# Attention and delta outputs split into two parts where they are made, in a one-core decoder layer on Trainium2

## The chip, the cores and the metric

One core of one Trainium2 chip runs the whole kernel. The time is device microseconds (us) of one execution of the program; the figure of a kernel is the median of several runs. Engines in the rows: PE is TensorE, PEld its weight loads, DVE VectorE, ACT ScalarE, POOL GpSimd, SP SyncE, which here issues all transfers between DRAM and the core's memory (SBUF).

## What is computed

One decoder layer on 1024 prompt positions and 8 x 8 sample positions, 1088 in all, with a model width of 1024. A half-step FFN comes first, then the mixer, then a second half-step FFN. The mixer, cut to what matters:

```python
qa, ka, va, qkvb, zb, ab, bb, ga, gb = split_columns(h @ w_in)
oa = sliding_window_attention(qa, ka, va)          # 512 columns
ob = gated_delta_net(conv(qkvb), ab, bb)           # 4 heads of 128
ob = rms_norm(ob, dn_out_norm) * silu(zb)          # 512 columns
merged = sigmoid(ga) * (oa @ w_branch_a) + sigmoid(gb) * (ob @ w_branch_b)
x = x + post2(merged @ w_out)
```

All of it is float32, and the outputs are the layer's x and the new caches and states.

## The kernel before, in words

Activations lie with features on the 128 partitions and positions along the free axis, in three column blocks c of 384, 384 and 320 positions (`CH`). Every large product is made of three matmuls of a faster float format: each operand is a pair, the part `hi` that the format holds and the rest `lo`, and `gemm` (lines 142 to 144) adds hi x hi, hi x lo and lo x hi. `split` (lines 194 to 196) makes such a pair: ScalarE copies into the short format (line 195), VectorE subtracts (line 196).

The mixer's stages overlap. Attention runs over the prompt (`attention_prompt`) and then over the sample (`attention_sample`), while `fill` feeds TensorE with matmuls of queued products: convolution inputs and the 16 gate blocks. The delta net follows in two pairs of heads (`Head`); their last step, `second`, normalizes the output `QK[:, cs]` block by block. In the DRAM tensors `oad` and `obd` (4 x 128 x 1088 float32 each) the attention and delta outputs wait for the branches. Gate blocks go through `gate_do`: product, tanh on ScalarE (line 931), store to `gd` (line 932). The last two gate blocks, 14 and 15, are drained for c = 0, 1, 2 directly before the branches.

The branch stage (lines 1511 to 1560) first loads `oad` and `obd` back, 24 pieces `o` of 128 x 384 or 320 (line 1519), and splits each into `oabh` and `oabl` (pairs `oab[c]`, j = 0 attention, j = 1 delta). Then `br(dd, w, c)` makes one of 8 output blocks dd for one column block: pA from the attention half of the weights, pB from the delta half, each 4 steps of 3 matmuls. Lines 1529 and 1530 load the gate blocks `ga` and `gb` from `gd` (both appear as a tile `t`), line 1531 makes (ga + 1) x pA, line 1532 (gb + 1) x pB, and 1533 to 1536 add them and split the result into `mh` and `ml`. pA and pB come from three rotating PSUM buffers `pa`. In the text, A0 and B0 are pA and pB of output block 0, and so on. The first four output blocks run over c = 0, then c = 1, c = 2, then the other four.

The order of the instructions on each engine is written out by the build: a scheduler places each instruction when its operands can be ready, transfers included, and every engine then runs its own list strictly in that order. A transfer that waits on SP holds all transfers behind it. Tile numbers in the order lists count instances, so `t_1303` is the tile of the last gate piece (gate 15, c = 2).

Of the kernel before, what the change touches and what calls it, by code (L numbers as in the profile page):

```python
# [7 lines left out]
F32 = mybir.dt.float32  # L8
F32R = mybir.dt.float32r
# [4 lines left out]
P = 128  # L14
KT = 8
NPR = 1024
NSM = 64
NT = NPR + NSM
# [17 lines left out]
def body(ctx: ExitStack, tc: tile.TileContext, d):  # L36
    nc = tc.nc
# [6 lines left out]
    dp = ctx.enter_context(tc.tile_pool(name="dp", bufs=1, space=bass.MemoryType.DRAM))  # L44
# [9 lines left out]
        return CH[c][1] - CH[c][0]  # L54

    xd = [dp.tile([P, KT, b - a], F32, tag=f"xd{c}", name=f"xd{c}") for c, (a, b) in enumerate(CH)]
    oad = dp.tile([4, P, NT], F32, tag="oad", name="oad")
    obd = dp.tile([4, P, NT], F32, tag="obd", name="obd")
    zd = dp.tile([4, P, NT], F32, tag="zd", name="zd")
    bm, bu = ([dp.tile([34, 32, 32], F32, tag=f"{n}{h}", name=f"{n}{h}") for h in range(4)] for n in ("bm", "bu"))  # L60

# [15 lines left out]
    def f32(ap):  # L77
        return ap.bitcast(F32)
# [3 lines left out]
    def uid(s):  # L82
        cnt[0] += 1
        return f"{s}_{cnt[0]}"
# [21 lines left out]
    def pb():  # L106
        turn[0] += 1
        return (ph, py)[turn[0] % 2]()
# [48 lines left out]
    def po_tile():  # L157
        return pp.tile([P, 512], F32, tag="po", name=uid("po"), bufs=1)
# [35 lines left out]
    def split(src, hi, lo):  # L194
        nc.scalar.copy(hi, src)
        nc.vector.tensor_tensor(out=lo, in0=src, in1=f32(hi), op=ALU.subtract)
# [357 lines left out]
    with tc.tile_pool(name="f1", bufs=12, side="left", reuse_waits="tile") as big1, tc.tile_pool(  # L554
        name="d1", bufs=4, side="right", reuse_waits="tile"
# [101 lines left out]
    YA = SL[2:6] + SL[0:2] + SL[6:8]  # L657
    HA = SL[8:16]
# [176 lines left out]
    def fill(us):  # L835
        while us > 0 and queue:
            t = next(queue[0], None)
            if t is None:
                queue.pop(0)
            else:  # L840
                us -= t
# [116 lines left out]
    def att_s(it):  # L958
        n, tp2 = items[it]
        k0 = 128 if n == 0 else 0  # L960
        ps = (ph(), py())
        for j in range(2):
            for g2, hs in enumerate(half2):
                mm = nc.tensor.matmul(
                    ps[g2][:, j * 256 + k0 : j * 256 + 256],
                    YA[tp2 * 2 + j][hs, n * P : n * P + P],
                    kT[hs, (n - 1) * P + k0 : (n + 1) * P],
                    start=True,
                    stop=True,
                )  # L970
                if masked:
                    tc.add_manual_dep(mm.ins, masked[-1], SYNC, reason="both halves start together")
        s4 = sbs[it % 2][:, :1024].rearrange("p (h k) -> p h k", k=256)[:, :, k0:256]
        with tc.high_priority(offset=10000):
            for g2 in range(2):
                mask = nc.vector.tensor_tensor(
                    out=s4[:, 2 * g2 : 2 * g2 + 2, :],
                    in0=ps[g2].rearrange("p (j k) -> p j k", k=256)[:, :, k0:256],
                    in1=cst[:, C_AM + k0 : C_AM + 256].unsqueeze(1).to_broadcast([P, 2, 256 - k0]),
                    op=ALU.add,  # L980
                )
            masked.append(mask.ins.name)
            softmax(s4, vec[:, V_SK + 4 * tp2 : V_SK + 4 * tp2 + 4], st())
# [38 lines left out]
    def attention_prompt():  # L1022
        n = len(items)
        for it in range(n + 2):
            if it < n:
                att_s(it)
            if it >= 2:
                att_v(it - 2)
            if 1 <= it <= n:
                att_t(it - 1)  # L1030
            fill(7.5 if it == 0 else 9.5 if it == n - 1 else 4.8)
        for t in range(4):
            nc.sync.dma_start(oad[t, :, :NPR], YA[t][:, :NPR])

    def attention_sample():
        kc, vc = YA[5], YA[7]
        nc.sync.dma_start(vc[:, :NPR].rearrange("p (b c) -> p b c", c=P), d["vc"].rearrange("b k c -> k b c"))
        nc.sync.dma_start(kc[:, :NPR].rearrange("p (b c) -> p b c", c=P), d["kc"])
        pos = po_tile()
        fill(3.0)  # L1040
        for it in range(4):
            bg2, g2 = it // 2, it % 2
            lo, hi = 64 * g2, 64 * g2 + 64
            ps = pb()
            for b4 in range(4):
                b = bg2 * 4 + b4
                ql = qs[lo:hi, b, :, :].rearrange("p t k -> p (t k)")
                nc.tensor.matmul(ps[32 * b4 : 32 * b4 + 32, 0:128], ql, kc[lo:hi, b * P : b * P + P], start=True, stop=True)
                nc.tensor.matmul(ps[32 * b4 : 32 * b4 + 32, 128:192], ql, kT[lo:hi, NPR:NT], start=True, stop=True)
            sb = YA[6][:, it * 256 : it * 256 + 192]  # L1050
            nc.vector.tensor_tensor(out=sb[:, 0:128], in0=ps[:, 0:128], in1=cst[:, C_SMC : C_SMC + P], op=ALU.add)
            nc.vector.tensor_tensor(
                out=sb[:, 128:192], in0=ps[:, 128:192], in1=cst[:, C_SMN + bg2 * NSM : C_SMN + bg2 * NSM + NSM], op=ALU.add
            )
            softmax(sb.unsqueeze(1), vec[:, V_SKS + g2 : V_SKS + g2 + 1], st())
        fill(13.0)
        ptbs = [YA[0][:, it * 256 : it * 256 + 256] for it in range(4)]
        for it in range(4):
            sb = YA[6][:, it * 256 : it * 256 + 192]
            pt = pb()  # L1060
            nc.tensor.transpose(pt[:, 0:128], sb[:, 0:128], ident)
            nc.tensor.transpose(pt[:NSM, 128:256], sb[:, 128:192], ident)
            nc.scalar.copy(ptbs[it][:, 0:128], pt[:, 0:128])
            nc.scalar.copy(ptbs[it][:NSM, 128:256], pt[:NSM, 128:256])
        fill(2.0)
        for it in range(4):
            bg2, g2 = it // 2, it % 2
            lo, hi = 64 * g2, 64 * g2 + 64
            ptb = ptbs[it]
            nc.tensor.matmul(  # L1070
                pos[lo:hi, bg2 * 128 : bg2 * 128 + 128], vts[:, lo:hi], ptb[:NSM, 128:256], start=True, stop=False
            )
            for b4 in range(4):
                b = bg2 * 4 + b4
                nc.tensor.matmul(
                    pos[lo:hi, bg2 * 128 + 32 * b4 : bg2 * 128 + 32 * b4 + 32],
                    vc[:, b * P + lo : b * P + hi],
                    ptb[:, 32 * b4 : 32 * b4 + 32],
                    start=False,
                    stop=b4 == 3,  # L1080
                )
        obs = YA[1][:, :256]
        nc.vector.tensor_copy(
            obs.rearrange("p (t b k) -> p t b k", t=4, b=8), pos[:, :256].rearrange("p (b t k) -> p t b k", t=4, b=8)
        )
        nc.sync.dma_start(oad[:, :, NPR:NT].rearrange("t p q -> p t q"), obs.rearrange("p (t q) -> p t q", t=4))


    ncv = s2b.tile([P, 12, 3], F32, tag="ncv", name="ncv")
# [23 lines left out]
    class Head:  # L1113
# [140 lines left out]
        def second(self, pks):  # L1254
            h = self.h
            q, L, v, M, k, U, QK, R = self.A
# [45 lines left out]
            w, cs, ix = chunk_of(8, h)  # L1302
# [27 lines left out]
            for c in range(8):  # L1330
                w, cs, ix = chunk_of(c, h)
                p = ps[c]
# [29 lines left out]
            p = pb()  # L1362
# [42 lines left out]
            for a, b in CH:  # L1405
                cs = slice(a, b)
                pq = pb()
                nc.tensor.matmul(pq[:, : b - a], ones, q[:, cs], start=True, stop=True)
                nc.scalar.activation(k[:, cs], pq[:, : b - a], AF.Identity, scale=1.0 / P, bias=eps4)
                nc.scalar.activation(v[:, cs], k[:, cs], AF.Abs_reciprocal_sqrt)  # L1410
                newton(v[:, cs], k[:, cs], M[:, cs])
                nc.vector.scalar_tensor_tensor(out=QK[:, cs], in0=QK[:, cs], scalar=hvd, in1=v[:, cs], op0=ALU.mult, op1=ALU.mult)
                nc.vector.tensor_tensor(out=QK[:, cs], in0=QK[:, cs], in1=U[:, cs], op=ALU.mult)
                nc.sync.dma_start(obd[h, :, cs], QK[:, cs])
                yield 0.0, 0.0

    def together(a, b):
# [39 lines left out]
    with tc.manual_schedule(engines={mybir.EngineType.PE}):  # L1457
# [7 lines left out]
        for hs in (heads[0:2], heads[2:4]):  # L1465
            a, b = hs
# [44 lines left out]
    dw2 = ctx.enter_context(tc.tile_pool(name="d2", bufs=4, side="right", reuse_waits="tile"))  # L1511
    oab = [pair(xp, c, "oab") for c in range(3)]
    m = [pair(big2, c, "m") for c in range(3)]
    for c, (a, b) in enumerate(CH):
        for j in range(2):
            hi, lo = oab[c][0][j], oab[c][1][j]
            for t in range(4):
                o = dw2.tile([P, 512], F32, tag=("dh", "dl")[t % 2], name=uid("o"))[:, : b - a]
                nc.sync.dma_start(o, (oad, obd)[j][t, :, a:b])
                split(o, hi[:, t, :], lo[:, t, :])  # L1520

    def br(dd, w, c):
        a, b = CH[c]
# [178 lines left out]
```

## Time and profile before

| | |
|---|---|
| median of 3 runs | 2398.41 us (2397.77 to 2401.87) |
| profiled execution | 2392.79 us, its span 2390.9 us |
| granted clock of TensorE, mean | 0.995 |
| TensorE busy | 2344.9 us (98%) |
| VectorE busy | 1697.5 us (71%) |
| ScalarE busy | 1112.6 us (47%) |
| DMA, mean | 116 GB/s, 35.9% of 16 engines' span |

The span is the part of the profiled execution that the trace covers; stretches below are in us from its start. TensorE is nearly always busy, so the views that tell something are the waits of PE, and around each of them the timelines of the engines that it waits for. Averages over the span hide the stages: the DMA's mean of 36% is made of stretches near full and of stretches near idle.

### The profile page before, as it was taken

To read this page: it belongs to the slowest core of one execution; us is meant where nothing else is said; L and a number is where in the kernel's file an instruction comes from. 1 tells how busy PE (TensorE), PEld (TensorE's weight loads), DVE (VectorE), ACT (ScalarE), POOL (GpSimd) and SP (SyncE) were. 2 spreads that over 40 slices of the span, in tenths; PEclk is the share of its full clock that TensorE was granted. 3 is DMA by queue.
4 is the path that set the end of the run, shared out by engine and by line. 5 is a ranking of instruction groups with operands and counts; after the bars stand their busy time and mean duration, and the time that the engine had idled before them with its cause. 6 is when DMAs were issued, how large, how long until landed. Compare 5 with 4: busy or idle time off the path is not lost. (4 is left out here: it accounts for less than half of the span.)

```text
span 2390.9 us, 38846 instructions
## 1 busy us (share of the span) xinstructions
PE 2344.9 (98%) x14535; PEld 2286.1 (96%) x14535; DVE 1697.5 (71%) x3453; ACT 1112.6 (47%) x2314; POOL 21.0 (1%) x21
## 2 busy tenths in 40 slices
PE   8999999999999999999999999999999999999997
PEld 7999999999999988899899999999999999999997
DVE  8887667677688567675598456588877667677677
ACT  7644323333366455552564453367644323333344
POOL 0000000000000000000000000000000000000000
PEclk9999999999999999999999999999999999999998
DMA  8332212212464420424322346456432212212453
GB/s 276 120 115 88 69 57 83 67 63 84 162 192 140 168 78 32 138 65 132 96 94 78 111 153 196 145 191 217 127 115 85 71 58 81 70 63 84 160 170 129
DMA packets 173828, 276.19 MB, mean 116 GB/s; under 512 B 35276, under 2 KB 76208, under 8 KB 173632
## 3 DMA queue, kind: packets, MB, share of 16 engines
q1 hardware_dynamic: 173640, 273.71, 35.9%
q8 instruction: 114, 1.87, 0.3%
q14 instruction: 74, 0.61, 0.1%
HBM read 231.22 MB, written 43.41 MB: 115 GB/s over the span
## 5 line engine op out<-in xcount | busy, mean ns | idle before, releaser
L466 PE MATMUL pa<-ch,h_c_s 128*128 128x384 f32 x704 | 236.4, 336 | 1.9 <-DVE t L472 1.6
L468 PE MATMUL pa<-ch,l_c_s 128*128 128x384 f32 x704 | 235.4, 334 | 0.0
L467 PE MATMUL pa<-cl,h_c_s 128*128 128x384 f32 x704 | 235.2, 334 | 0.0
L472 DVE TENSOR_TENSOR t<-pa,t 128x384 f32<-128x384 f32 x308 | 170.6, 554 | 88.6 <-PE pa L468 88.4
L466 PE MATMUL pa<-ch,h_c_a 128*128 128x384 f32 x528 | 177.1, 335 | 0.5 <-DVE t L472 0.3
L468 PE MATMUL pa<-ch,l_c_a 128*128 128x384 f32 x528 | 176.7, 335 | 0.0
L467 PE MATMUL pa<-cl,h_c_a 128*128 128x384 f32 x528 | 176.6, 334 | 0.0
L115 ACT CAST h_c_a<-r_c_a 128x512 fp32r<-128x512 f32 x132 | 81.8, 620 | 128.0 <-PE pa L467 110.7
L466 PEld LDWEIGHTS pa<-ch,h_c_s 128*128 128x128 f32 x704 | 132.2, 188 | 5.2 <-DVE t L472 5.0
L115 ACT CAST h_c_s<-q_c_s 128x512 fp32r<-128x512 f32 x132 | 82.0, 622 | 108.5 <-PE pa L467 95.4
L467 PEld LDWEIGHTS pa<-cl,h_c_s 128*128 128x128 f32 x704 | 132.2, 188 | 0.0
L468 PEld LDWEIGHTS pa<-ch,l_c_s 128*128 128x128 f32 x704 | 132.2, 188 | 0.0
L142 PE MATMUL pa<-xbh,h_ga 128*128 128x384 f32 (+1 forms) x384 | 129.1, 336 | 0.0
L144 PE MATMUL pa<-xbh,l_ga 128*128 128x384 f32 (+1 forms) x384 | 126.1, 328 | 0.0
L143 PE MATMUL pa<-xbl,h_ga 128*128 128x384 f32 (+1 forms) x384 | 126.0, 328 | 0.0
L466 PEld LDWEIGHTS pa<-ch,h_c_a 128*128 128x128 f32 x528 | 99.1, 188 | 1.5 <-DVE t L472 1.0
L467 PEld LDWEIGHTS pa<-cl,h_c_a 128*128 128x128 f32 x528 | 99.1, 188 | 0.0
L468 PEld LDWEIGHTS pa<-ch,l_c_a 128*128 128x128 f32 x528 | 99.1, 188 | 0.0
L115 ACT CAST h_c_s<-r_c_s 128x512 fp32r<-128x512 f32 x44 | 27.4, 622 | 148.8 <-PE pa L467 139.2
L142 PE MATMUL pa<-xbh,h_qkv 128*128 128x384 f32 (+1 forms) x288 | 95.2, 331 | 0.0
L144 PE MATMUL pa<-xbh,l_qkv 128*128 128x384 f32 (+1 forms) x288 | 93.9, 326 | 0.0
L143 PE MATMUL pa<-xbl,h_qkv 128*128 128x384 f32 (+1 forms) x288 | 93.9, 326 | 0.0
(627 smaller groups left out, 7253.5 us busy)
## 6 DMA issues: line engine op xcount, KB each, us to landing
r_c_a<-in_up_dram SPq DMA_DIRECT2D x132, 256.0 KB
r_wo<-in_wo_dram SPq DMA_DIRECT2D x48, 256.0 KB
q_c_a<-in_up_dram SPq DMA_DIRECT2D x44, 256.0 KB
q_ub<-in_up_dram SPq DMA_DIRECT2D x44, 256.0 KB
r_ub<-in_up_dram SPq DMA_DIRECT2D x44, 256.0 KB
r_ua<-in_up_dram SPq DMA_DIRECT2D x42, 256.0 KB
q_ua<-in_up_dram SPq DMA_DIRECT2D x42, 256.0 KB
r_da<-in_dn_dram SPq DMA_DIRECT2D x40, 256.0 KB
```

The lines of the kernel that those rows point to most:

```text
L115: nc.scalar.copy(hi, full)
L142: nc.tensor.matmul(ps[:, :n], hi[:, j, :], at(xh, k), start=first, stop=False)
L143: nc.tensor.matmul(ps[:, :n], hi[:, j, :], at(xl, k), start=False, stop=False)
L144: mm = nc.tensor.matmul(ps[:, :n], lo[:, j, :], at(xh, k), start=False, stop=last)
L466: nc.tensor.matmul(ps, wh[:, k, :], xh[:, k, :], start=k == 0, stop=False)
L467: nc.tensor.matmul(ps, wh[:, k, :], xl[:, k, :], start=False, stop=False)
L468: nc.tensor.matmul(ps, wl[:, k, :], xh[:, k, :], start=False, stop=k == 3)
L472: nc.vector.tensor_tensor(out=out, in0=ps, in1=other, op=ALU.add)
```

## The change

`oad` and `obd` become pairs of DRAM tensors, hi and lo. The outputs are split where they are made: four splits of 128 x 1024 at the end of `attention_prompt`, one of 128 x 256 at the end of `attention_sample`, and one for each head and column block at the end of `second`, 12 in all, into buffers that are free there. Each store becomes two. At the branches the parts are loaded directly into `oabh` and `oabl`, one transfer for each block c, half j and part, 12 in all, and the 24 splits there are gone.

```diff
@@ -54,8 +54,8 @@
         return CH[c][1] - CH[c][0]
 
     xd = [dp.tile([P, KT, b - a], F32, tag=f"xd{c}", name=f"xd{c}") for c, (a, b) in enumerate(CH)]
-    oad = dp.tile([4, P, NT], F32, tag="oad", name="oad")
-    obd = dp.tile([4, P, NT], F32, tag="obd", name="obd")
+
+    oad, obd = ([dp.tile([4, P, NT], F32, tag=f"{n}{i}", name=f"{n}{i}") for i in "hl"] for n in ("oa", "ob"))
     zd = dp.tile([4, P, NT], F32, tag="zd", name="zd")
     bm, bu = ([dp.tile([34, 32, 32], F32, tag=f"{n}{h}", name=f"{n}{h}") for h in range(4)] for n in ("bm", "bu"))
 
@@ -1030,7 +1030,11 @@
                 att_t(it - 1)
             fill(7.5 if it == 0 else 9.5 if it == n - 1 else 4.8)
         for t in range(4):
-            nc.sync.dma_start(oad[t, :, :NPR], YA[t][:, :NPR])
+            parts = (HA[3], HA[4]) if t % 2 == 0 else (HA[6], HA[7])
+            hi, lo = (x[:, :NPR].bitcast(F32R) for x in parts)
+            split(YA[t][:, :NPR], hi, lo)
+            for dst, x in zip(oad, (hi, lo)):
+                nc.sync.dma_start(dst[t, :, :NPR], f32(x))
 
     def attention_sample():
         kc, vc = YA[5], YA[7]
@@ -1083,7 +1087,10 @@
         nc.vector.tensor_copy(
             obs.rearrange("p (t b k) -> p t b k", t=4, b=8), pos[:, :256].rearrange("p (b t k) -> p t b k", t=4, b=8)
         )
-        nc.sync.dma_start(oad[:, :, NPR:NT].rearrange("t p q -> p t q"), obs.rearrange("p (t q) -> p t q", t=4))
+        hi, lo = (YA[1][:, o : o + 256].bitcast(F32R) for o in (256, 512))
+        split(obs, hi, lo)
+        for dst, x in zip(oad, (hi, lo)):
+            nc.sync.dma_start(dst[:, :, NPR:NT].rearrange("t p q -> p t q"), f32(x).rearrange("p (t q) -> p t q", t=4))
 
 
     ncv = s2b.tile([P, 12, 3], F32, tag="ncv", name="ncv")
@@ -1411,7 +1418,10 @@
                 newton(v[:, cs], k[:, cs], M[:, cs])
                 nc.vector.scalar_tensor_tensor(out=QK[:, cs], in0=QK[:, cs], scalar=hvd, in1=v[:, cs], op0=ALU.mult, op1=ALU.mult)
                 nc.vector.tensor_tensor(out=QK[:, cs], in0=QK[:, cs], in1=U[:, cs], op=ALU.mult)
-                nc.sync.dma_start(obd[h, :, cs], QK[:, cs])
+                hi, lo = q[:, cs].bitcast(F32R), k[:, cs].bitcast(F32R)
+                split(QK[:, cs], hi, lo)
+                for dst, x in zip(obd, (hi, lo)):
+                    nc.sync.dma_start(dst[h, :, cs], f32(x))
                 yield 0.0, 0.0
 
     def together(a, b):
@@ -1513,11 +1523,8 @@
     m = [pair(big2, c, "m") for c in range(3)]
     for c, (a, b) in enumerate(CH):
         for j in range(2):
-            hi, lo = oab[c][0][j], oab[c][1][j]
-            for t in range(4):
-                o = dw2.tile([P, 512], F32, tag=("dh", "dl")[t % 2], name=uid("o"))[:, : b - a]
-                nc.sync.dma_start(o, (oad, obd)[j][t, :, a:b])
-                split(o, hi[:, t, :], lo[:, t, :])
+            for i in range(2):
+                nc.sync.dma_start(f32(oab[c][i][j]), (oad, obd)[j][i][:, :, a:b].rearrange("t p q -> p t q"))
 
     def br(dd, w, c):
         a, b = CH[c]
```

Line numbers after the change are larger by 3 to 10: line 1033 becomes 1037, 1131 becomes 1138, 1414 becomes 1424, 1519 becomes 1527, 1529 to 1536 become 1536 to 1543.

SP, from the last c = 0 load of the branches to the first gate loads. Before (`o` are the pieces that were split, `t<-gd` with line 1529 the gate blocks ga):

```order
L932 DMA gd<-t_1303_15181 128x320
L1519 DMA o_15279<-obd 128x384
L1519 DMA o_15283<-oad 128x320
L1519 DMA o_15287<-oad 128x320
L1519 DMA o_15291<-oad 128x320
L1519 DMA o_15295<-oad 128x320
L1519 DMA o_15299<-obd 128x320
L1519 DMA o_15303<-obd 128x320
L1519 DMA o_15307<-obd 128x320
L1519 DMA o_15311<-obd 128x320
L1529 DMA t_1330_15389<-gd 128x384
L1529 DMA t_1334_15424<-gd 128x384
```

Now, with the first load of ga on line 1536:

```order
L1527 DMA oabl_1_15251<-obl 128x4x384
L932 DMA gd<-t_1303_15234 128x320
L1527 DMA oabh_0_15252<-oah 128x4x384
L1527 DMA oabl_0_15254<-oal 128x4x384
L1527 DMA oabh_1_15253<-obh 128x4x384
L1527 DMA oabl_1_15255<-obl 128x4x384
L1527 DMA oabh_0_15256<-oah 128x4x320
L1527 DMA oabl_0_15258<-oal 128x4x320
L1527 DMA oabh_1_15257<-obh 128x4x320
L1527 DMA oabl_1_15259<-obl 128x4x320
L1536 DMA t_1306_15358<-gd 128x384
L1536 DMA t_1310_15393<-gd 128x384
```

Between the store of the last gate piece and the first load of ga stood 9 transfers, 1.5 MB; there are now 8 transfers of 5.8 MB, all of the blocks c = 1 and c = 2.

VectorE at the first branch products. Before (line 196 is the subtract of a split, 1532 consumes B0 and then B1, 1531 A0):

```order
L196 TENSOR_TENSOR oabl_1_15202<-o_15275,oabh_1_15200 128x384
L1532 SCALAR_TENSOR_TENSOR t_1331_15390<-t_1331_15390,pa_15364 128x384
L196 TENSOR_TENSOR oabl_1_15202<-o_15279,oabh_1_15200 128x384
L196 TENSOR_TENSOR oabl_0_15205<-o_15283,oabh_0_15203 128x320
L196 TENSOR_TENSOR oabl_0_15205<-o_15287,oabh_0_15203 128x320
L196 TENSOR_TENSOR oabl_0_15205<-o_15291,oabh_0_15203 128x320
L196 TENSOR_TENSOR oabl_0_15205<-o_15295,oabh_0_15203 128x320
L196 TENSOR_TENSOR oabl_1_15206<-o_15299,oabh_1_15204 128x320
L196 TENSOR_TENSOR oabl_1_15206<-o_15303,oabh_1_15204 128x320
L1532 SCALAR_TENSOR_TENSOR t_1335_15425<-t_1335_15425,pa_15399 128x384
```

Now (1539 consumes B0 and B1, 1538 A0 and A1, line 116 splits a weight tile):

```order
L672 SCALAR_TENSOR_TENSOR t_1303_15234<-pa_15209,r_8289 128x320
L116 TENSOR_TENSOR l_br_1_15329<-r_br_1_15326,h_br_1_15328 128x512
L1539 SCALAR_TENSOR_TENSOR t_1307_15359<-t_1307_15359,pa_15333 128x384
L1539 SCALAR_TENSOR_TENSOR t_1311_15394<-t_1311_15394,pa_15368 128x384
L1538 SCALAR_TENSOR_TENSOR t_1306_15358<-t_1306_15358,pa_15332 128x384
L1538 SCALAR_TENSOR_TENSOR t_1310_15393<-t_1310_15393,pa_15367 128x384
```

The splits between the two steps that free B0's and B1's buffers are gone; the order of those steps among themselves is as it was.

SP at the end of prompt attention. Before (`s<-gcd` loads the decay sums of the first delta head):

```order
L1131 DMA s_8354<-gcd 128x1088
L1033 DMA oad<-s_8342 128x1024
L1033 DMA oad<-s_8343 128x1024
L1033 DMA oad<-s_8344 128x1024
L901 DMA out_cvo_dram<-sn_10694 128x27
L932 DMA gd<-t_896_10709 128x320
L1033 DMA oad<-s_8345 128x1024
```

Now (line 1138 is that load):

```order
L1037 DMA oal<-s_8354 128x1024
L1037 DMA oah<-s_8356 128x1024
L932 DMA gd<-t_896_10711 128x320
L1037 DMA oah<-s_8353 128x1024
L1037 DMA oal<-s_8357 128x1024
L1037 DMA oal<-s_8354 128x1024
L1037 DMA oah<-s_8356 128x1024
L1037 DMA oal<-s_8357 128x1024
L932 DMA gd<-t_907_10855 128x384
L932 DMA gd<-t_909_10883 128x384
L1138 DMA s_8356<-gcd 128x1088
```

The load of the decay sums stood ahead of the four stores; it now stands behind all eight, because it goes into a buffer that a part is stored from.

## Rows read from the trace of the kernel before

**Rows 1.** The page, part 1: engine, busy us (share of the span) x instructions.

```profile
PE 2344.9 (98%) x14535; PEld 2286.1 (96%) x14535; DVE 1697.5 (71%) x3453; ACT 1112.6 (47%) x2314; POOL 21.0 (1%) x21
```

**Rows 2.** Waits of PE, 1390 to 1500: total us, times, longest us.

```profile
PE pa L142 <- DVE t L1532: 3.1, 2, 2.2
```

**Rows 3.** Timeline of PE at the branches: start us, us, instruction [idle before <-releaser].

```profile
1431.44 0.34 PE L142 MATMUL pa<-oabh,h_br 128*128 128x384 f32 x1
...
1433.55 0.33 PE L142 MATMUL pa<-oabh,h_br 128*128 128x384 f32 x1
...
1438.74 0.44 PE L142 MATMUL pa<-oabh,h_br 128*128 128x384 f32 x1 [0.86 <-DVE t L1532]
...
1443.33 0.44 PE L142 MATMUL pa<-oabh,h_br 128*128 128x384 f32 x1 [2.22 <-DVE t L1532]
...
1446.09 0.52 PE L142 MATMUL pa<-oabh,h_br 128*128 128x384 f32 x1
1446.41 0.52 PE L143 MATMUL pa<-oabl,h_br 128*128 128x384 f32 x1
...
1449.17 0.33 PE L142 MATMUL pa<-oabh,h_br 128*128 128x384 f32 x1
```

**Rows 4.** Timeline of DVE, same stretch.

```profile
1434.39 3.83 DVE L196 TENSOR_TENSOR oabl<-o,oabh 128x384 fp32r<-128x384 f32 x8
...
1442.73 0.55 DVE L1532 SCALAR_TENSOR_TENSOR t<-t,pa 128x384 f32<-128x384 f32 x1
...
1449.58 0.56 DVE L1532 SCALAR_TENSOR_TENSOR t<-t,pa 128x384 f32<-128x384 f32 x1 [1.62 <-DMA t<-gd]
```

**Rows 5.** Windows: us, PE PEld DVE ACT POOL busy, PEclk, DMA share, GB/s.

```profile
1437.00:1443.00 6.00, 3.25 (x18) 2.61 (x16) 5.09 (x12) 4.01 (x9) 0.00 (x0) 1.00 0.89 264
1443.00:1450.00 7.00, 6.67 (x29) 6.67 (x30) 4.86 (x11) 1.45 (x3) 0.00 (x0) 0.76 0.89 290
```

**Rows 6.** Timeline of SP, 1434 to 1447: start us, us, issue.

```profile
1434.56 0.32 SPq L932 DMA_DIRECT2D gd<-t  x1
...
1437.64 2.21 SPq L1519 DMA_DIRECT2D o<-obd  x4
1439.90 1.84 SPq L1529 DMA_DIRECT2D t<-gd  x4
1441.79 1.38 SPq L130 DMA_DIRECT2D r_br<-in_wbr_dram  x3
1446.12 0.80 SPq L1530 DMA_DIRECT2D t<-gd  x2
```

**Rows 7.** Groups by line and shape, 1395 to 1500: busy us, mean ns | idle before.

```profile
L196 DVE TENSOR_TENSOR oabl<-o,oabh 128x384 fp32r<-128x384 f32 x16 | 8.1, 552 | 3.7 <-ACT oabh L195 3.7
L195 ACT CAST oabh<-o 128x384 fp32r<-128x384 f32 x16 | 7.9, 511 | 5.2 <-DMA o<-oad 3.6 <-DMA o<-obd 1.4
```

**Rows 8.** Timeline of ACT, 1434 to 1444.

```profile
1434.06 0.47 ACT L931 ACTIVATE t<-t 128x320 f32<-128x320 f32 x1
...
1443.70 0.46 ACT L195 CAST oabh<-o 128x320 fp32r<-128x320 f32 x1 [0.97 <-DMA o<-obd]
```

**Rows 9.** Windows, the same columns, during the stores of attention.

```profile
1000.00:1002.00 2.00, 2.00 (x13) 2.00 (x12) 1.21 (x6) 0.49 (x1) 0.00 (x0) 1.00 1.02 415
```

**Rows 10.** Timelines of SP, DVE, ACT and PE, 995 to 1021.

```profile
995.52 0.33 SPq L1131 DMA_DIRECT2D s<-gcd  x1
995.94 2.87 SPq L1033 DMA_DIRECT2D oad<-s  x3
...
1001.45 0.35 DVE L1139 SCALAR_TENSOR_TENSOR s<-s,tk_gc,cst 128x128 f32<-128x128 f32 x1 [0.59 <-DMA s<-gcd]
...
1018.02 0.26 ACT L1063 COPY s<-ph 128x128 f32<-128x128 f32 x1
...
1020.44 0.43 PE L1070 MATMUL po<-s,vts 64*64 64x128 f32 x2
```

**Rows 11.** Waits of PE, 1185 to 1210, the end of the first pair of heads.

```profile
PE py L1408 <- ACT s L1409: 0.9, 1, 0.9
```

## The prediction, made before the changed kernel ran

> **What bounds the kernel now.** The page's busy table is read first: TensorE is busy for 98% of the span [rows 1], so a cost or a gain counts only where it makes or removes a TensorE wait. Next, the waits of PE around the branches: two waits, 3.1 us in all, both ended by DVE's line 1532 [rows 2]. Then the timelines there. TensorE starts the branch products at 1431.44, and a half product (12 matmuls: attention half A or delta half B of one output block) takes 1433.55 - 1431.44 = 2.1 us [rows 3]. Four output blocks give A0 B0 A1 B1 A2 B2 A3 B3 on three PSUM buffers: B1 takes B0's buffer, A2 takes B1's, B2 takes A0's, each once VectorE has consumed it. B0 and B1 are consumed by line 1532 with gate values loaded long before, A0 by line 1531 with gate 0 (`ga`). The waits at 1438.74 and 1443.33 are B1 and A2, whose releaser stood among the splits of line 196 on DVE, 3.83 us of them in one row, the second line 1532 at 1442.73 [rows 3, 4]. After them matmuls run at half clock: 1.00 before, 0.76 granted over 1443 to 1450 [rows 5]. A3 starts at 1449.17 [rows 3]. Six half products without a wait would put it at 1431.44 + 6 x 2.1 = 1444.0; the branches therefore lose 5.2 us, 3.1 of waits and the rest half clock. That is all a better start of the branches can give back: 0.22% of the time. A measurement of this kernel tells about 0.2%, or 4.8 us, from no change.
>
> The other thing to read there is the DMA: share 0.89 at 264 and 290 GB/s through the stage [rows 5]. The stage is already close to a full transfer queue, and the loads of gate values stand behind the branch loads in SP's order [rows 6].
>
> **The change, part by part.**
> *Splits removed at the branches.* 24 splits go: 16 at 0.511 + 0.552 us [rows 7] and 8 smaller ones. Removed from DVE and ACT they are worth no time by themselves, since neither engine is the bound; what they give is the two waits above. In the new order DVE has lines 1539 for B0 and B1 directly behind the gate tails, so B1 starts on time and A2 waits well under 1 us. Worth 3.1 us of waits, and 2.1 of half clock if nothing replaces them: -5.2 us at most.
>
> *Loads doubled, in twelve large transfers.* All the branch input was 24 x 192 or 160 KB, 4.46 MB; now it is 8.91 MB, four loads for each column block c. The block that TensorE needs first (c0) is four loads; those of c1 and c2 are 4 x 786,432 + 4 x 655,360 bytes (128 partitions x 4 x 384 or 320 numbers) = 5.77 MB. In the order list SP now does: the last c0 load, the store of the last gate (tile t_1303), the eight loads of c1 and c2, and only then the four loads of ga, the first for A0. Two facts set when ga 0 arrives.
>
> First, the store of t_1303 cannot go before ScalarE's tanh of it. Before, that tanh ran at 1434.06, and the store went at 1434.56, 0.5 us later [rows 6, 8]. The gate product ends when the branches begin, 1431.44 [rows 3]; with ACT's casts gone I take the tanh at 1432.0 and the store and the first of the eight loads at 1432.5 (bounds 1431.9 and 1434.6, that is the product's end + 0.5 and the row of before).
>
> Second, 5.77 MB go ahead of ga 0. I take 280 GB/s, between the 264 and 290 of the stage itself [rows 5]: 20.6 us (19.9 to 21.9). The last c0 load (0.79 MB) is still on its way when they are issued, and ga 0 itself is 0.2 MB; less the time that SP needs to issue, I add 2.4 us for both and for the latency: ga 0 lands at 1432.5 + 20.6 + 2.4 = 1455.5. That transfers are served about in the order of issue I read from before: two gate loads issued at 1446.12, behind 0.79 MB of weights issued from 1441.79, were used at 1449.58, after DVE had waited 1.62 us for one, and the last of the split loads, issued by 1439.85, was cast at 1443.70, when ACT had waited for it 0.97 us [rows 4, 6, 8].
>
> From its landing VectorE's line 1538 and TensorE's restart take 0.6 us (1442.73 to 1443.33 for the same step, [rows 3, 4]). So B2 starts at 1456.1 instead of 1446.09 [rows 3], after a wait of about 13 us. A3 follows 2.1 us later, 1458.2. The long idle time will cost half clock again: after a wait of 2.2 us the cost before was 2.1, I take 1.7 (bounds 0 and 3.5, that is 24 matmuls each 0.32 us behind the last, 1446.41 less 1446.09, instead of 2.1 / 12 = 0.176 [rows 3]). A3 then starts at 1459.9 against 1449.17: **+10.7 us**. Later loads (ga 1 to 3 right behind, the next gb, the weights) land within 5 us of ga 0, before their products come; c1 and c2 are there by then. Nothing behind the wait catches up, because TensorE is the bound to the end.
>
> The far bound of the rate is the highest stretch read, 415 GB/s during the attention stores [rows 9]: 13.9 us instead of 20.6, ga 0 at 1448.8, A3 at about 1453.2, +4.0 us.
>
> The Trainium skill, "DMA: Bandwidth & Descriptors", section "Bandwidth", says to batch to 1 MiB or more, and measures 341 GB/s at 1 MB against 138 at 64 KB; that speaks for the larger loads. By its 341 the eight loads would take an estimated 16.9 us and the whole change would come to about +7 instead of +10.7. The stage of before moves 264 to 290 GB/s at a share of 0.89 [rows 5], and a 768 KB load here still consists of the same runs of 1,536 bytes, so I keep the rate of the rows.
>
> *Splits added at the sources.* After prompt attention: 4 casts and 4 subtracts of 128x1024 (by [rows 7] scaled to the width, an estimated 1.4 us each, 5.5 on either engine), 8 stores of 512 KB instead of 4 (three of them from 995.94 [rows 10]). TensorE runs through that stretch on queued convolution and gate work, which is the cover. One thing is behind: SP's load of a delta head's decay sums (`gcd`) went ahead of the stores at 995.52 and was used at 1001.45 [rows 10]; it now goes behind all eight stores, 4.2 MB, at 280 to 415 GB/s 10 to 15 us. ScalarE's exponentials of these sums then stand ahead of the copies of the sample's probabilities (1018.02), for which TensorE comes at 1020.44 [rows 10]. I expect the load at 1015 to 1018 and a wait of 0 to 1.5 us: **+0.5**.
> *Head ends.* 12 splits and 12 more stores. At the first pair's end PE waits 0.9 us for ACT's line 1409 now [rows 11]; a split of 0.51 + 0.55 us in ACT's and DVE's queue [rows 7] can double it or lie beside it. Zero taken, 0 to 1 as bounds. At the second pair's end the gate products cover it.
>
> **Sum:** 10.7 + 0.5 = +11.2 us. The profiled execution took 2392.8 us, 5.6 below the median of 2398.4; against it the change gives 2404.0, and against the median **2409.6 us**, slower by 0.47%.
>
> **Rivals.**
> *Gate loads are not held back (not slower).* If the engines serve ga 0 before the big loads end, the two old waits go and nothing replaces them. It decides at the landing of ga 0: by 1440 the gain of 5.2 is kept but for some 0.7 of A2, giving 2393.2 to 2393.9; break-even is a landing at 1449.17 - 2.1 - 0.6 = 1446.5 without half clock, 1444.8 with it. For it: the program needs the big loads of c2 last, and they have slack. Against: in the order list ga 0 is issued behind them, and the reading above of loads served in order; to bring 5.77 MB ahead of 1446.5 takes 500 GB/s. Chance 0.14.
> *The loads run faster.* 340 to 415 GB/s give +4 to +7, with no attention wait 2402 to 2405, half of it within the measurement's 0.2%. For it the 415 [rows 9], against it the share of 0.89 at 290 [rows 5]. Chance 0.14.
> *More is late than ga 0.* The attention wait grows to 3 us because the decay sums land after 1018, or the head ends cost 1, or half clock lasts longer: 2412 to 2415. Chance 0.12.
>
> **How the numbers follow.** My forecast (one wait for ga 0 at B2, +7 to +14) has 0.60. Slower by over 0.2% (above 2403.2): 0.54 of it, the third rival's 0.12 and half of the second, 0.07, together 0.73. Within: 0.06 of the forecast (the runs of before themselves spread over 4 us), the other half of the second, and 0.06 of the first, 0.19. Faster (below 2393.6): the rest of the first, 0.08. The range takes the forecast with its bounds, the second rival and of the first the landings up to break-even: 2396 to 2415.
>
> **What would show it.** In the new trace: no line 196 between 1425 and 1450; a wait of TensorE of 10 to 15 us before B2, ended by line 1538, which itself waits for the load of t from gd; ga loads issued after the eight big ones and landing near 1455; DMA share near 0.9 from 1432 to 1455; half clock behind the wait. I am wrong if that wait is under 4 us, if the loads run above 350 GB/s, or if TensorE waits several us in the attention stage, between 1000 and 1025.

## The result, and the profile after

| | before | after |
|---|---|---|
| median, runs of the same comparison (12 each) | 2395.93 us | 2405.39 us |
| lowest to highest | 2391.85 to 2401.87 | 2403.55 to 2409.09 |
| profiled execution, its span | 2392.79, 2390.9 | 2403.55, 2401.5 |

The changed kernel is slower: ratio 1.0040, 95% interval 1.0033 to 1.0048, that is 9.5 us. The forecast was 2409.6 us, 11.2 above the median then shown (2398.41, 2.5 above the one in this table), with slower by over 0.2% at 0.73.

The page's busy line of after, beside [rows 1], shows that no engine has much more or less to do:

```profile
PE 2344.9 (98%) x14535; PEld 2286.9 (95%) x14535; DVE 1696.4 (71%) x3446; ACT 1109.3 (46%) x2307; POOL 21.9 (1%) x21
```

TensorE's 2344.9 us are the same to the tenth. The time is lost between instructions, so the next view is the waits of PE in after, 1380 to 1500, beside [rows 2]:

```profile
PE pa L142 <- DVE t L1538: 9.1, 1, 9.1
PE pa L142 <- DVE t L1539: 0.7, 1, 0.7
PE pa L143 <- DMA oabl<-obl: 0.6, 1, 0.6
```

The two waits of before, 3.1 us, are gone, and one of 9.1 us has come, ended by line 1538, which consumes A0 with ga 0. The timelines of SP, DVE and PE of after, beside [rows 3, 4, 6]:

```profile
1432.36 0.32 SPq L932 DMA_DIRECT2D gd<-t  x1
1432.77 0.39 SPq L1527 DMA_DIRECT2D oabh<-oah  x1
...
1440.67 1.77 SPq L1527 DMA_DIRECT2D oabl<-obl  x1
1442.49 3.77 SPq L1536 DMA_DIRECT2D t<-gd  x4
...
1440.80 0.55 DVE L1539 SCALAR_TENSOR_TENSOR t<-t,pa 128x384 f32<-128x384 f32 x1 [2.45 <-PE pa L144]
1452.19 1.02 DVE L1538 SCALAR_TENSOR_TENSOR t<-t,pa 128x384 f32<-128x384 f32 x2 [10.84 <-DMA t<-gd]
...
1435.56 0.44 PE L143 MATMUL pa<-oabl,h_br 128*128 128x384 f32 x1 [0.58 <-DMA oabl<-obl]
...
1441.50 0.41 PE L142 MATMUL pa<-oabh,h_br 128*128 128x384 f32 x1 [0.74 <-DVE t L1539]
...
1452.89 0.66 PE L142 MATMUL pa<-oabh,h_br 128*128 128x384 f32 x1 [9.07 <-DVE t L1538]
1453.35 0.52 PE L143 MATMUL pa<-oabl,h_br 128*128 128x384 f32 x1
...
1458.15 0.45 PE L143 MATMUL pa<-oabl,h_br 128*128 128x384 f32 x1
1458.44 0.34 PE L144 MATMUL pa<-oabh,l_br 128*128 128x384 f32 x1
```

Read from the top: the store of the last gate piece, the eight loads, the four loads of ga behind them. VectorE has nothing to do from 1441.35 until ga 0 lands at 1452.19; TensorE's B2 starts 0.7 us later, and 16 matmuls run 0.32 us apart until 1458.15. The windows of after, beside [rows 5]:

```profile
1434.00:1440.00 6.00, 5.42 (x30) 4.83 (x29) 0.55 (x1) 0.00 (x0) 0.00 (x0) 1.00 1.02 349
1440.00:1446.00 6.00, 3.08 (x17) 2.47 (x15) 0.55 (x1) 0.00 (x0) 0.00 (x0) 1.00 1.06 368
1446.00:1452.00 6.00, 0.00 (x0) 0.00 (x0) 0.00 (x0) 0.00 (x0) 0.00 (x0) 0.68 1.07 369
1452.00:1455.00 3.00, 2.11 (x7) 2.14 (x8) 2.81 (x7) 0.94 (x2) 0.00 (x0) 0.50 0.95 332
```

From 1434 to 1452 the transfers run at 349 to 369 GB/s and a share of 1.02 to 1.07; in the last six of these us TensorE, VectorE and ScalarE all stand still. The granted clock falls in that idle stretch (0.68 on average) and is 0.50, half clock, at the restart.

How much the stage takes as a whole is best read from the groups of line 142: the first start of the branch products and of the products with w_out behind them (columns: count, then duration min/median/max in ns, first to last start). Before:

```profile
L142 PE MATMUL pa<-oabh,h_br x192: 306/334/522, 1431.4 to 1531.0; 128*128 128x384 f32 x128, 128*128 128x320 f32 x64
L142 PE MATMUL pa<-mh,h_wo x192: 309/334/630, 1531.4 to 1629.4; 128*128 128x384 f32 x128, 128*128 128x320 f32 x64
```

After:

```profile
L142 PE MATMUL pa<-oabh,h_br x192: 306/334/659, 1431.1 to 1539.4; 128*128 128x384 f32 x128, 128*128 128x320 f32 x64
L142 PE MATMUL pa<-mh,h_wo x192: 309/334/637, 1539.9 to 1638.1; 128*128 128x384 f32 x128, 128*128 128x320 f32 x64
```

The branch stretch took 1531.4 - 1431.4 = 100.0 us and takes 108.8: +8.8. The waits account for 10.4 - 3.1 = 7.3 of it. Of the 1.5 left, half clock makes about 0.9: it cost 2.4 us in after (below) and 1.5 in before, where 11 steps from 1444.83 to 1448.30 took 3.47 instead of 11 x 0.176 = 1.94. The rest is not placed. Up to the branches the two kernels are 0.3 us apart. Behind the branches after is 2.1 us longer; that code is unchanged, and the same stretch differs by up to 3.7 us among the kernels below, so it is left out of the reading.

In the attention stage TensorE does not wait at all between 1000 and 1025. The timelines of SP and ACT of after there, beside [rows 10]:

```profile
1010.32 0.32 SPq L1138 DMA_DIRECT2D s<-gcd  x1
...
1014.85 0.63 ACT L1155 ACTIVATE s<-s 128x512 f32<-128x512 f32 x1 [1.22 <-DMA s<-gcd]
```

The load of the decay sums went from 995.52 to 1010.32, its use from 1001.45 to 1014.85, and that is still in time for the sample's products. The transfers were busy there too: 305 to 342 GB/s at a share of 0.82 to 0.93 from 1000 to 1015.

### The profile page after: what moved, and what is told of

It is laid out like the page before. It is cut to its first block, busy times and chain, and to the rows that moved or that the text cites. A ratio compares the mean times of both kernels' runs of the same rounds, so it can differ in the third digit from the quotient of the medians.

```text
span 2401.5 us, 38844 instructions
## 1 busy us (share of the span) xinstructions
PE 2344.9 (98%) x14535; PEld 2286.9 (95%) x14535; DVE 1696.4 (71%) x3446; ACT 1109.3 (46%) x2307; POOL 21.9 (1%) x21
```

## The experiments

Two theories. **Queue:** ga 0 is late because it is issued behind 5.77 MB of loads that nobody needs yet, and transfers are served about in order. **Bytes:** the change doubles what the branches load, the transfer engines are full, and something is late in whatever order. The stretch is that from the first branch product to the first with w_out.

| run | us | before, same chip | ratio, 95% | stretch |
|---|---|---|---|---|
| after | 2405.39 | 2395.93 | 1.0033 to 1.0048 | 108.8 |
| e1_gates_first | 2402.02 | 2396.15 | 1.0012 to 1.0040 | 104.2 |
| e2_c2_late | 2398.98 | 2396.15 | 1.0002 to 1.0021 | 101.1 |
| e3_small_loads | 2404.96 | 2396.15 | 1.0026 to 1.0056 | 109.8 |
| e4_big_on_act | 2400.82 | 2396.15 | 1.0000 to 1.0032 | 101.8 |
| e5_before_reordered | 2392.40 | 2398.23 | 0.9966 to 0.9988 | 95.5 |
| e6_gates_first_c2_late | 2399.71 | 2398.23 | 0.9994 to 1.0014 | 100.9 |
| e7_c0_high | 2399.03 | 2398.23 | 0.9994 to 1.0012 | 102.7 |
| e8_attention_half | 2389.94 | 2396.27 | 0.9967 to 0.9984 | 96.7 |

**e1_gates_first: ga ahead of the eight loads.** `load_oab(c)` holds the four loads of block c; `br` takes its `ga` from `early`.

```diff
+    load_oab(0)
+    for dd in range(4):
+        early[dd] = t1()
+        nc.sync.dma_start(early[dd][:, :384], gd[dd, :, 0:384])
+    load_oab(1)
+    load_oab(2)
...
```

> The changed kernel, with the four loads of ga for column block 0 placed ahead of the eight loads of blocks 1 and 2; bytes and everything else the same. Queue theory (ga 0 is late because it is issued behind 5.77 MB and transfers are served in order): the wait of 9.1 us before B2 goes to under 1 us, but the load of gb for output block 2 still stands behind the eight loads, so a wait of 3 to 7 us appears at the first product of column block 1 (about 1447 us), ended by the line that consumes gb; time 2400 to 2403 us. Byte theory (the stage has too many bytes for the DMA, whatever their order): the wait before B2 stays 6 us or more, time 2404 to 2407.

The waits of PE of this run, 900 to 1500:

```profile
PE pa L142 <- DVE t L1551: 4.8, 1, 4.8
...
PE pa L143 <- DMA oabl<-obl: 1.7, 1, 1.7
```

The wait before B2 is gone, and 4.8 us have come for gb (line 1551), whose load still stood behind the eight. TensorE waited for it from 1454.3 to 1459.1, later than I wrote. With the same bytes the wait follows the transfer that is put last: the queue theory holds for what is late. The wait for the last load of block 0 has grown from 0.6 to 1.7.

**e2_c2_late: 3.15 MB instead of 5.77 ahead of ga.** Blocks 0 and 1 are loaded where all three were, block 2 here:

```diff
...
                 br(q4 * 4 + i, ws[i], c)
+                if q4 == 0 and c == 0 and i == 3:
+                    load_oab(2)
```

> The changed kernel, with the four loads of column block 2 issued behind the loads of ga, so that 3.15 MB instead of 5.77 MB stand ahead of ga 0. Queue theory: ga 0 lands 2.62 MB / 0.36 MB per us = 7 to 8 us earlier, near 1444.5; wait before B2 0 to 2 us, hardly any half clock, time 2395 to 2398. Byte theory: a wait of 5 us or more stays before B2 or comes soon behind it, time 2402 or more.

The timelines of SP and DVE:

```profile
1433.69 0.39 SPq L1528 DMA_DIRECT2D oabh<-oah  x1
...
1446.43 1.02 DVE L1542 SCALAR_TENSOR_TENSOR t<-t,pa 128x384 f32<-128x384 f32 x2 [3.59 <-DMA t<-gd]
```

From the issue of the first large load to the use of ga 0 it is 12.7 us, in after 1452.19 - 1432.77 = 19.4. For 2.62 MB less, 6.7 us less: 390 GB/s, close to the 360 that was expected. PE's wait there is 1.8 us instead of 9.1. The time, 2399, is a little above the expected range, with 3.7 us of waits left.

**e3_small_loads: the same order, 48 loads.**

```diff
-                nc.sync.dma_start(f32(oab[c][i][j]), (oad, obd)[j][i][:, :, a:b].rearrange("t p q -> p t q"))
+                for t in range(4):
+                    nc.sync.dma_start(f32(oab[c][i][j][:, t, :]), (oad, obd)[j][i][t, :, a:b])
```

> The changed kernel, with each load of parts cut into four (48 loads of 192 or 160 KB instead of 12 of 768 or 640), in the same order. If the rate does not hang on the size of a transfer, the eight old loads take the same 16 us at 350 to 370 GB/s, the wait before B2 is 8 to 10 us and the time 2404 to 2407. If small transfers run at the 264 to 290 GB/s that the kernel before showed with them, ga 0 lands 4 to 6 us later: wait 13 to 15 us, time 2409 to 2412.

The windows of this run:

```profile
1434.00:1440.00 6.00, 4.68 (x24) 3.78 (x23) 0.56 (x1) 0.00 (x0) 0.00 (x0) 1.00 0.97 314
1440.00:1446.00 6.00, 5.17 (x29) 4.56 (x27) 0.56 (x1) 0.00 (x0) 0.00 (x0) 1.00 1.03 363
1446.00:1452.00 6.00, 0.00 (x0) 0.00 (x0) 0.00 (x0) 0.00 (x0) 0.00 (x0) 0.75 1.03 340
```

The wait is 10.3 us, a little above the 8 to 10 of the first expectation, and the time is that of after. Transfers of 160 to 192 KB run at 314 to 363 GB/s, so the 264 to 290 of [rows 5] were not a limit that such transfers have.

**e4_big_on_act: the eight loads issued by ScalarE.**

```diff
-                nc.sync.dma_start(f32(oab[c][i][j]), (oad, obd)[j][i][:, :, a:b].rearrange("t p q -> p t q"))
+                (nc.sync if c == 0 else nc.scalar).dma_start(f32(oab[c][i][j]), (oad, obd)[j][i][:, :, a:b].rearrange("t p q -> p t q"))
```

> The changed kernel, with the eight loads of column blocks 1 and 2 issued by ScalarE instead of SyncE; same bytes at about the same time, but ga is no longer behind them in the list of one engine. If what delays ga is its place in SyncE's list, ga 0 lands within some 5 us of its issue near 1430, no wait over 1 us before B2, time 2393 to 2398. If all transfers share one order or the DMA is simply full, a wait of 5 us or more stays, time 2402 to 2406.

The timelines of SP, ACT, PE and DVE:

```profile
1432.95 1.21 SPq L1536 DMA_DIRECT2D t<-gd  x1
...
1432.52 0.38 ACTq L1527 DMA_DIRECT2D oabh<-oah  x1
1436.06 0.37 ACTq L1527 DMA_DIRECT2D oabl<-oal  x1
...
1441.54 0.69 PE L143 MATMUL pa<-oabl,h_br 128*128 128x384 f32 x1 [3.48 <-DMA oabl<-obl]
...
1442.70 0.56 DVE L1538 SCALAR_TENSOR_TENSOR t<-t,pa 128x384 f32<-128x384 f32 x1 [6.06 <-DMA t<-gd]
```

Neither expectation met it. The wait before B2 is gone, and ga 0 was used 9.5 us earlier than in after (1442.70 against 1452.19). But it was issued at 1432.95, so it still took 9.7 us, and the last load of block 0 now makes B0 wait 3.5 us. The transfers ran at 365 to 393 GB/s between 1434 and 1446, the eight loads among them: a place in another engine's list frees ga 0 from the queue, but not from sharing the transfer engines. That ScalarE's loads took from the last load of block 0 what it needed first is my reading; it is the byte theory, for the part that the order does not explain.

**e5_before_reordered: the kernel before with the order of e1 and e2.** Here `load_oab(c)` holds the eight loads of `o` and their splits.

```diff
+    load_oab(0)
+    for dd in range(4):
+        early[dd] = t1()
+        nc.sync.dma_start(early[dd][:, :384], gd[dd, :, 0:384])
+    load_oab(1)
...
+                if q4 == 0 and c == 0 and i == 3:
+                    load_oab(2)
```

> The kernel before, splits at the branches and all, with only the order changed: the four loads of ga for column block 0 ahead of block 1, and the eight split loads of block 2 behind the first four output blocks of block 0. If the 5.2 us that the branches lose before are due to splits standing ahead of the steps that free PSUM buffers, fewer of them stand there now: waits of 0 to 1.5 us at the branches, the stretch from the first branch product to the first product with w_out 95 to 97.5 us instead of 100.0, time 2391 to 2394. If they are due to transfers that arrive late, about 100 and 2396.

The waits of PE of this run, 1380 to 1500:

```profile
PE po L1344 <- DVE s L1336: 0.2, 1, 0.2
PE pa L143 <- DVE oabl L196: 0.2, 1, 0.2
```

All 24 splits and the single loads are there, and the branches wait 0.2 us. The stretch is 95.5 us, 4.5 less than before, and the kernel is faster by 0.23%. What the branches lost before came from the order, not from the splits' work. VectorE's timeline in before, right behind the first row of [rows 4]:

```profile
1438.14 0.55 DVE L1532 SCALAR_TENSOR_TENSOR t<-t,pa 128x384 f32<-128x384 f32 x1
1438.94 1.83 DVE L196 TENSOR_TENSOR oabl<-o,oabh 128x384 fp32r<-128x384 f32 x4 [0.26 <-ACT oabh L195]
1441.34 1.48 DVE L196 TENSOR_TENSOR oabl<-o,oabh 128x320 fp32r<-128x320 f32 x3 [0.56 <-ACT oabh L195]
```

Ahead of the first freeing step (1438.14) stand 3.83 us of splits without a gap, ahead of the second (1442.73) seven more with 0.8 us of gaps, in which VectorE waited for casts. So the place of the splits is the larger part there; since e5 moves loads and splits together, the share of loads that came late to a split is not separated.

**e6_gates_first_c2_late: the changed kernel in the same order** (e1 and e2 together).

> The changed kernel, with ga of block 0 ahead of block 1 and the loads of block 2 behind the gb loads: both delays of ga and of gb that the first runs showed should go. Queue theory: the wait for the last load of block 0 (0.6 to 1.7 us) stays, no other wait over 1 us, the stretch from the first branch product to the first with w_out 96 to 98 us instead of 108.8, time 2392 to 2395. Byte theory: waits of 3 us or more in all, 99 or more, time 2396 or more.

The timelines of SP and PE:

```profile
1431.93 0.52 SPq L1530 DMA_DIRECT2D oabl<-obl  x1
1435.04 0.32 SPq L932 DMA_DIRECT2D gd<-t  x1
1435.41 6.02 SPq L1535 DMA_DIRECT2D t<-gd  x4
...
1440.70 0.69 PE L143 MATMUL pa<-oabl,h_br 128*128 128x384 f32 x1 [2.75 <-DMA oabl<-obl]
```

ga and gb no longer make TensorE wait, and the stretch falls from 108.8 to 100.9. It does not reach the 96 to 98 of the queue theory, and stretch and time are as the byte theory had them: the last part of block 0 was issued at 1431.93 and used 8.8 us later, B0 waited 2.75 us, and the clock was 0.50 from 1440 to 1446. But the transfers were not full while TensorE waited (the last two columns are share and GB/s):

```profile
1438.00:1440.00 2.00, 0.00 (x0) 0.00 (x0) 0.00 (x0) 0.00 (x0) 0.00 (x0) 0.99 0.42 135
1440.00:1442.00 2.00, 1.30 (x4) 1.30 (x5) 0.35 (x1) 0.00 (x0) 0.00 (x0) 0.50 0.30 106
```

From 1420 to 1438 the share was 0.95 to 1.07, and only then did it fall. Of the 16 landings that the trace has for this load, 15 had come by 1438.68 and the last came at 1440.66. So about 2.0 of the 2.75 us go to one late sixteenth of the load, which neither theory has; why it was late is not shown. Beside e5, the same order with the splits at the branches, the change costs 5.4 us.

**e7_c0_high: block 0 placed earlier in SP's list.**

```diff
-    load_oab(0)
+    with tc.high_priority(offset=20000):
+        load_oab(0)
```

> As the run before it, with the four loads of block 0 placed earlier in SP's list, ahead of the last stores of the delta outputs and of the gates. If the wait for the last load of block 0 comes from its place behind those stores, it goes, and the stretch is 95 to 96.5 us, time 2391 to 2394. If the earlier loads hold up gate stores or the tiles that wait for them, a wait of 1 us or more shows on TensorE ahead of the branches, between 1405 and 1431 us, and the time is no better than that of the run before it.

The waits of PE, 1380 to 1500:

```profile
PE pa L142 <- DVE t L1550: 3.7, 1, 3.7
PE pa L142 <- DVE t L672: 1.3, 1, 1.3
```

The wait for block 0 is gone, and two others have come, inside the branches (the first ends at 1438.93) and not ahead of them as I wrote: the stores of the gates now go behind, so the tile of the last gate piece (line 672) and then gate values (line 1550) are late. The time is that of e6, the stretch 1.8 us longer. Something is late in each order tried with all of the change.

**e8_attention_half: e6 with the parts for attention alone.** The stores of the delta outputs are shown; at the branches these are loaded in pieces and split as before.

```diff
-                hi, lo = q[:, cs].bitcast(F32R), k[:, cs].bitcast(F32R)
-                split(QK[:, cs], hi, lo)
-                for dst, x in zip(obd, (hi, lo)):
-                    nc.sync.dma_start(dst[h, :, cs], f32(x))
+                nc.sync.dma_start(obd[0][h, :, cs], QK[:, cs])
```

> The changed kernel in the order of e6_gates_first_c2_late, with the change made for attention alone: its parts are stored and loaded as in the changed kernel, the delta outputs are stored whole and split at the branches as before. In that order all of the change took 100.9 us from the first branch product to the first with w_out, and none of it (e5_before_reordered) 95.5, which leaves 5.4 for the parts. If it is the bytes near the start of the branches that cost these 5.4 us, half of them are gone: wait before B0 0 to 1.5 us, the stretch 95.5 to 98, time 2391 to 2396. If it is the delta half's late stores and loads alone, the wait is gone and the stretch is 95 to 96, time 2391 to 2393.5. If any load of 768 KB ahead of a needed one costs it, the stretch stays over 99.

The waits of PE, 1380 to 1500:

```profile
PE pa L142 <- DVE t L1553: 1.4, 2, 0.7
```

TensorE waits for no load directly any more, though the first of the two waits, at 1438.28, ends at a step of VectorE that stood behind a split, and the cast of that split had waited 4.15 us for a piece of the delta outputs. The stretch is 96.7, within the first expectation, and the kernel is faster than before by 0.25%. It is the fastest run, but its interval and that of e5 overlap, so the attention half of the change costs no time that can be told, and no gain of it is shown. Of the 5.4 us of e6, 100.9 - 96.7 = 4.2 come with the delta half, whose stores and loads fall together in the last 20 us ahead of the branches. Whether the doubled stores or the doubled loads of that half weigh more was not tried, so this names the half that costs and not the mechanism.

## Why the prediction was right or wrong

*Which way, where and why: right.* One wait of TensorE before B2, ended by line 1538, which waits for ga 0 behind eight loads of 5.77 MB. e1, e2 and e6 move that wait with the order and with the bytes ahead.

*The first of the eight loads at 1432.5: right.* It went at 1432.77, behind the gate store at 1432.36.

*The rate, 280 GB/s: the step that failed, in size.* The loads ran at 349 to 369, ga 0 landed at 1452.2 instead of 1455.5, and the wait was 9.1 us instead of about 13. I read the share of 0.89 in [rows 5] as a queue near its limit; after shows 1.02 to 1.07. The stage of before was slower for another reason. Its loads went into a few `o` buffers that a split had to free: between 1434 and 1446 SP waited four times, 1.2 us in all, for a subtract of line 196 before it could issue one. Whether that is the whole reason is not shown; e3 shows that it was not the size of the transfers. By my own sign, loads above 350 GB/s, this step was wrong: two of the three windows show 368 and 369. The 2.4 us for the rest were too few: the eight loads at 349 to 369 take 15.6 to 16.5 us, and from the issue of the first to the use of ga 0 it was 19.4. The Trainium skill, "DMA: Bandwidth & Descriptors", section "Bandwidth", measures 341 GB/s at 1 MB and 138 at 64 KB, for loads issued from GpSimd. The first is nearer than my 280 to what ran here; the second no run here shows, as loads of 160 to 192 KB still ran at 314 to 363 (e3).

*Half clock after the wait, 1.7 us: a little low.* The 16 steps from 1452.89 to 1458.15 took 5.26 us instead of 16 x 0.176 = 2.82, so 2.4 us were lost, within the stated bounds. The 2.1 that I read as half clock in before are 1.5 of half clock and 0.6 of something else.

*A wait at A2 well under 1 us: about right* (0.7). *The last load of block 0:* in my sum it was only a part of what stands ahead of ga. It made B0 wait 0.6 us itself, and in the better orders (e4, e6) it became the bound.

*Attention +0.5, head ends 0: nothing was lost there.* The decay sums were used at 1014.85, a little ahead of the 1015 to 1018 that I expected, and the wait of 0.9 us of [rows 11] stands in after too, at the same size.

*The sum.* The errors of size are in part opposite: ga 0 came 3.3 us earlier, half clock cost 0.7 more, and the branches of after began 0.3 us earlier than those of before, which makes 10.7 - 3.3 + 0.7 + 0.3 = 8.4. The wait of B0 adds nothing here, because TensorE would have stood for ga 0 in its place. Measured: 8.8 at the branches against 10.7, 9.5 in all against 11.2. That the whole came so near is partly luck: attention cost nothing of its 0.5, and the profiled executions differ by 2.1 us behind the branches, which no term of the sum had. The rival with faster loads, +4 to +7, had the better rate, but the same 2.4 us for the rest and the same half clock, and came out too low.

## What to carry to other kernels

Before moving work off an engine, ask whether its amount or its place in the engine's list makes others wait: here the same splits and loads cost 4.5 us more in one order than in another. A larger load placed ahead of a small one that is needed sooner delays it by its bytes over the rate; write down for each load when it is needed, and issue in that order. Storing and loading two parts doubles the traffic, and what that costs is decided by who waits for it, not by how busy the transfers are: after attention they were busy too (shares of 0.82 to 0.93), and nothing that TensorE needed was late; at the end of the delta net, where the branches follow at once, the doubled traffic cost 4.2 us even in the better order.

## What the runs showed of the hardware that I had not expected

TensorE fell to half clock without any wait, among the narrow state products of the delta net, and not at the same place in each trace. Windows of after and then of before, at the end of the first pair of heads and at that of the second:

```profile
1180.00:1182.00 2.00, 2.00 (x9) 1.87 (x9) 0.00 (x0) 0.18 (x1) 1.25 (x1) 0.50 0.83 286
...
1390.00:1392.00 2.00, 2.00 (x16) 1.91 (x15) 0.00 (x0) 0.76 (x2) 2.00 (x2) 1.00 0.64 198
```

```profile
1180.00:1182.00 2.00, 2.00 (x15) 1.96 (x15) 0.43 (x2) 0.69 (x3) 1.69 (x1) 1.00 1.01 327
...
1390.00:1392.00 2.00, 2.00 (x7) 1.85 (x8) 0.00 (x0) 0.26 (x1) 1.32 (x1) 0.50 0.59 149
```

PE is busy 2.00 of 2.00 us in all four, at 0.50 in one place in after and in the other in before. Ahead of both falls stand products of 128x16 and 64x64 between the gate products. With the matmuls of the two traces counted off against each other, the start in after less the start in before goes from -0.74 to 2.32 us at the first place and from 2.79 to -0.30 at the second: each fall costs 3.1 us. Of the ten traces the eight with some part of the change fall near 1180, before and e5 do not; before and e3 to e7 fall near 1390. With one trace for each kernel it is not shown whether the change brings the fall near 1180. Single executions of one kernel differ by more than one such fall, so a change of a few us in this kernel is read from the stretch that it touches, and only then from the whole time.
